# Two K units of every gate and up projection pair in seven products, the residual kept in device memory, and ScalarE's own silu and gelu

## The chip, the core and the metric

The kernel runs on one core of a Trainium2 chip. The metric is the device time of one execution in microseconds (us). The core's engines are TensorE (PE, matrix products; PEld is its weight load), VectorE (DVE), ScalarE (ACT), GpSimd (POOL) and SyncE (SP, which here only issues DMAs). Each engine, and each engine's queue of DMA issues, works through its own list of instructions in order. They wait for each other on semaphores.

## What is computed

Two layers of a gated decoder trunk, all float32, over 256 positions with 2048 channels. Weights are read once.

```python
def reference(x, mix_norm, w_in, ..., w_gate, w_up, w_down):
    for l in range(DEPTH):                       # 2 layers
        h = rms_norm(x, mix_norm[l])
        q, k, v, uv, gate_logits = split(h @ w_in[l])            # 2048 x 7680
        branch_a = sliding_window_attention(rope(norm(q)), rope(norm(k)), v, sinks[l]) @ w_attn_branch[l]
        branch_b = chunked_sgu(jax.nn.gelu(uv), ...) @ w_sgu_branch[l]
        gates = jax.nn.sigmoid(gate_logits)
        x = x + (gates[..., :D] * branch_a + gates[..., D:] * branch_b) @ w_out[l]
        h2 = rms_norm(x, ffn_norm[l])
        x = x + (jax.nn.silu(h2 @ w_gate[l]) * (h2 @ w_up[l])) @ w_down[l]    # 2048 x 5632, 5632 x 2048
    return x
```

## The kernel before

**Work and jobs.** The whole program is a list of jobs. A job multiplies the 256 x K activations by a weight block of 1024 columns (two column blocks of 512, called c = 0 and 1) and runs over K in units of 512. A feed-forward gate or up job has K = 2048, so four units. Activations are held transposed, split into a high and a low float32r part (`uh`, `ul`). Each weight piece is split the same way: ScalarE copies it rounded into `whi` (`high`, L241), VectorE subtracts to get `wlo` (`low`, L249), and TensorE does three matmuls (`three`, L368 to L370): hi x hi, lo x hi, hi x lo.

**Whole units and units in seven products.** A whole unit is four parts (two K halves by two column blocks); one part is 12 matmuls. In a job with `m` units in Strassen form, these come first: seven products `11, t1, t2, 21, t3, 22, t4` of one K half and one column block each, six matmuls a part. Four of the seven need a difference of weight pieces (`add`, L224, VectorE). `Job.m` is the number of such units. With two units the products interleave: 11 of unit 0, 11 of unit 1, t1 of unit 0 and so on. When a product's last unit is done, ScalarE copies one accumulation bank into another (L402): after `11`, after `t2`, and after `t3` into the bank on which `t4` then accumulates. After `21` it copies a bank to `p5`, and after `22` VectorE adds that into two banks (L408). A job in Strassen form holds all five accumulation banks.

**Order.** The order is written by hand: `Stream` hands out the parts and is called for each (`next`, `fill`). It emits splits of up to five parts ahead (N_LOW = 5 `wlo` buffers, N_HIGH = 6 `whi` buffers), and the weight sums some parts further ahead. `after(n, fn)` puts work n slots later (a whole part is one slot, a product half a slot). `evicting` does the work on a finished job's banks: for c = 0 at once, for the second column block spread over the next job.

**Weight loads.** Each unit's 512 x 1024 weights come as two DMAs of 1 MB (the two K halves) into `raw` buffers, of which there are four (N_RAW = 4). SP issues them all (L203), each when the buffer's last reader is done.

**Feed-forward.** Eleven column blocks f in three rounds (0 to 3, 4 to 7, 8 to 10). A round runs a gate job and an up job per pair of f, then two down jobs that add into the residual. Round three ends with one job that holds gate and up of f = 10. `xs` (128 x 2 x 2048) holds the residual in SBUF throughout. The gate eviction is a tanh on ScalarE (L1072) and a multiply on VectorE (L1076); the up eviction is one VectorE multiply (L1084). Gelu in the mixers is a square, a copy, a tanh on ScalarE and two VectorE multiplies.

```python
class Stream:
    def load(self):
        while len(self.raws) < len(loads):
            n = len(self.raws) - N_RAW
            if n >= 0 and last_use[n] >= len(self.parts):
                return
            self.fetch()
```

Of the kernel before, what the change touches and what calls it, by code (L numbers as in the profile page):

```python
# [33 lines left out]
N_RAW = 4  # L34
N_HIGH = 6
N_LOW = 5
N_BIG = 24
G_BUSY, G_LAND = 3.5, 3
T1_LATE, THEN_LATE = 1.5, 3
# [4 lines left out]
M_OUT, M_FFN, M_DOWN = (0, 1), 1, 1  # L44
M_Q = 0
M_GATE, M_ATT, M_SGU = (0, 1, 1, 1), (0, 0), (0, 0)
GELU_A = 0.044715
GELU_C = 0.7978845608028654
# [3 lines left out]
def hybrid_trunk(ctx: ExitStack, tc: tile.TileContext, x, mix_norm, w_in, q_norm, k_norm, sinks,  # L52
# [3 lines left out]

    const = ctx.enter_context(tc.tile_pool(name="const", bufs=1))
# [3 lines left out]
    wsum = ctx.enter_context(tc.tile_pool(name="wsum", bufs=1))  # L61
# [81 lines left out]
    for l in range(DEPTH):  # L143
# [13 lines left out]
        for fs in ROUNDS:  # L157
            for f in fs[::2]:
                if f + 1 < NF:
                    for w in (w_gate, w_up):  # L160
                        add_job([w[l, :, f * CW:(f + 2) * CW]], m=M_FFN)
                else:
                    add_job([w[l, :, f * CW:(f + 1) * CW] for w in (w_gate, w_up)], m=M_FFN)
            for o in (0, CW2):
                add_job([w_down[l, :, o:o + CW2]], units=list(fs), m=M_DOWN)
# [131 lines left out]
    def evicting(c, fn, then=None, ahead=None):  # L297
# [8 lines left out]
        else:  # L306
            late = behind(1, T1_LATE)
# [5 lines left out]
            if then is not None:  # L313
                after(behind(2, THEN_LATE), then)
# [13 lines left out]
    xs = const.tile([P, NT, D], F32, name="xs")  # L328
    for c in range(NCH):
        for t in range(NT):  # L330
            nc.sync.dma_start(xs[:, t, c * CW:(c + 1) * CW],
# [239 lines left out]
    class Norm:  # L571
# [15 lines left out]
        def squares(self, c):  # L587
            for t in range(NT):
                junk = temp(name="junk")
                nc.scalar.activation(junk, xs[:, t, c * CW:(c + 1) * CW], AF.Square,  # L590
                                     accum_out=self.ss[t][:, c:c + 1])

        def unit(self, c, on_pe=False, sums=False, at_once=False):
            transposed(self.units, c, xs[:, :, c * CW:(c + 1) * CW], cols=self.cols[:, 4 * c:4 * c + 4],
                       on_pe=on_pe, sums=sums, at_once=at_once)

        def finish(self):
            self.r, self.rh, self.rr = [], [], []
# [8 lines left out]
            def rest():  # L607
                for t in range(NT):
                    rh = tiny(1, f"rhalf{t}", 2)
                    nc.vector.tensor_scalar(out=rh, in0=self.r[t], scalar1=0.5, scalar2=None, op0=ALU.mult)  # L610
                    rr = tiny(1, f"rr{t}", 2)
                    nc.vector.tensor_tensor(out=rr, in0=self.r[t], in1=rh, op=ALU.mult)
                    self.rh.append(rh)
                    self.rr.append(rr)
# [263 lines left out]
    class Spatial:  # L878
# [6 lines left out]
        def gelu(self, c, ps, dst):  # L885
            sq = slot([P, NT, CW], name="sq")

            def evicted(t):
                nc.scalar.activation(sq[:, t, :], ps[t], AF.Square, scale=self.nrm.r[t])
                nc.scalar.activation(dst[:, t, :], ps[t], AF.Copy, scale=self.nrm.rh[t])  # L890

            def inner():
                nc.vector.scalar_tensor_tensor(out=flat(sq), in0=flat(sq), scalar=1.0 / GELU_A, in1=flat(dst),
                                               op0=ALU.add, op1=ALU.mult)

            def tanh():
                nc.scalar.activation(sq, sq, AF.Tanh, scale=2.0 * GELU_C * GELU_A)

            def outer():
                nc.vector.scalar_tensor_tensor(out=flat(dst), in0=flat(sq), scalar=1.0, in1=flat(dst),  # L900
                                               op0=ALU.add, op1=ALU.mult)

            evicting(c, lambda t: None, ahead=evicted)
            for i, fn in enumerate((inner, tanh, outer)):
                calm(1 + i, fn)
# [56 lines left out]
    def residual(units, nxt, sums, out_at=None, scale=None):  # L962

        for j in range(0, NCH, 2):

            def done(c, ps, j=j):
                o = j + c

                def then():
                    nxt.unit(o, sums=sums and o == 0)  # L970
                    after(5 if c == 0 else 2, lambda: nxt.squares(o))
                    if o == NCH - 1:
                        after(3, lambda: nxt.finish())

                evicting(c, lambda t: added(o, t, ps), then if nxt is not None else None)
# [163 lines left out]
```

## Time and profile before

| | |
|---|---|
| median of 3 runs | 2468.36 us (2466.8 to 2468.55) |
| the profiled execution's own time | 2468.03 us |
| its span, first to last instruction | 2466.3 us |
| busy: PE, PEld, DVE, ACT, POOL | 100%, 82%, 77%, 56%, 19% of the span |
| granted TensorE clock | 1.000 |
| weights and the rest moved by DMA | 507.73 MB, mean 206 GB/s |

A timeline row gives start, length, engine, line, operation, out<-in, and in brackets the idle time before it and who ended it. `x3` means three such instructions in a row. Matmul ends are modelled, so a matmul's own time is read from the distance between two starts.

### The profile page before, as it was taken

How to read it: one execution, taken by the hardware profiler on the slowest of the kernel's cores; microseconds unless marked ns; L12 is line 12 of the kernel's file. 1: busy time of each engine (PE TensorE's matmuls, PEld its weight loads, DVE VectorE, ACT ScalarE, POOL GpSimd, SP SyncE). 2: the span in 40 equal slices, each digit the busy share in tenths (PEclk: the TensorE clock that was granted, in tenths of full speed). 3: DMA queues.
4: the chain of work that ended last, by engine and by line, in shares of the span. 5: the costliest groups of instructions: out<-in, count | busy, mean ns of one | idle time of the engine just before them, and what ended most of it. 6: DMA issues, size and time to landing. Idle time of an engine off the chain costs nothing.

```text
span 2466.3 us, 30726 instructions
## 1 busy us (share of the span) xinstructions
PE 2455.4 (100%) x11046; PEld 2029.3 (82%) x11046; DVE 1887.3 (77%) x2107; ACT 1373.3 (56%) x1688; POOL 470.7 (19%) x903
## 2 busy tenths in 40 slices
PE   9999999999999999999999999999999999999999
PEld 8888888888888888888888888888888888888887
DVE  6797675797977687778867976757878776977696
ACT  6565455476655555555655554544756555655554
POOL 1411300541220022002235022014402200220020
PEclk9999999999999999999999999999999999999999
DMA  8644656766565557566766456566756665665564
GB/s 295 221 156 159 213 172 221 221 217 228 204 220 190 206 204 239 171 229 199 230 235 216 156 169 207 189 195 201 252 187 239 205 208 202 206 223 189 203 205 153
DMA packets 162730, 507.73 MB, mean 206 GB/s; under 512 B 22912, under 2 KB 25584, under 8 KB 162576
## 3 DMA queue, kind: packets, MB, share of 16 engines
q1 hardware_dynamic: 134512, 477.05, 57.7%
q0 software_dynamic: 27744, 28.44, 3.8%
q8 instruction: 86, 1.41, 0.2%
q14 instruction: 68, 0.56, 0.1%
q10 hardware_dynamic: 320, 0.27, 0.0%
HBM read 475.27 MB, written 2.10 MB: 194 GB/s over the span
## 4 chain that ended last, share of the span: by engine, by line
PE 98%; DVE 1%; DMA 0%; ACT 0%; issue 0%; POOL 0%; DVEq 0%; ACTq 0%; POOLq 0%
PE acc L368 32%; PE acc L369 32%; PE acc L370 32%; PE po L864 1%; PE psc L822 1%; DMA tt<-blk 0%; PE ppt L853 0%; PE psg L949 0%; DVE wlo L249 0%; PE pt L533 0%; PE pwarm L346 0%; POOL tt L460 0%; DVE sums L491 0%; DVE blk L454 0%; DVE ul L519 0%
## 5 line engine op out<-in xcount | busy, mean ns | idle before, releaser
L249 DVE TENSOR_TENSOR wlo<-raw,whi 128x1024 fp32r<-128x1024 f32 (+1 forms) x940 | 1132.8, 1218 | 486.1 <-PE acc L369 398.1
L241 ACT ACTIVATE whi<-raw 128x1024 fp32r<-128x1024 f32 (+1 forms) x940 | 983.4, 1057 | 823.1 <-PE acc L370 746.3
L368 PE MATMUL acc<-whi,uh 128*128 128x512 f32 x3164 | 1240.0, 392 | 2.2 <-DVE gate L1043 1.5
L370 PE MATMUL acc<-whi,ul 128*128 128x512 f32 x3164 | 1233.0, 390 | 0.5 <-DVE ul L561 0.5
L369 PE MATMUL acc<-wlo,uh 128*128 128x512 f32 x3164 | 1232.8, 390 | 0.7 <-DVE wlo L249 0.7
L460 POOL DMA_DIRECT2D tt<-blk x800 | 392.2, 497 | 1715.4 <-DVE blk L454 959.7
L368 PEld LDWEIGHTS acc<-whi,uh 128*128 128x128 f32 x3164 | 594.3, 188 | 130.6 <-ACT acc L402 2.7
L370 PEld LDWEIGHTS acc<-whi,ul 128*128 128x128 f32 x3164 | 594.2, 188 | 124.9 <-DVE ul L561 1.0
L369 PEld LDWEIGHTS acc<-wlo,uh 128*128 128x128 f32 x3164 | 594.5, 188 | 122.1 <-DVE wlo L249 1.4
L368 PE MATMUL acc<-whi,sh 128*128 128x512 f32 x336 | 131.0, 390 | 0.8 <-ACT acc L402 0.8
L370 PE MATMUL acc<-whi,sl 128*128 128x512 f32 x336 | 130.9, 390 | 0.0
L369 PE MATMUL acc<-wlo,sh 128*128 128x512 f32 x336 | 130.9, 389 | 0.0
L241 ACT ACTIVATE whi<-sum 128x1024 fp32r<-128x1024 f32 x84 | 89.0, 1059 | 72.7 <-PE acc L370 56.7
L249 DVE TENSOR_TENSOR wlo<-sum,whi 128x1024 fp32r<-128x1024 f32 x84 | 102.6, 1222 | 13.4 <-ACT whi L241 11.0
L402 ACT ACTIVATE acc<-acc 128x512 f32<-128x512 f32 x126 | 74.4, 590 | 21.7 <-PE acc L370 19.8
L368 PEld LDWEIGHTS acc<-whi,sh 128*128 128x128 f32 x336 | 63.1, 188 | 14.3 <-ACT acc L402 1.2
L370 PEld LDWEIGHTS acc<-whi,sl 128*128 128x128 f32 x336 | 63.1, 188 | 13.1
L369 PEld LDWEIGHTS acc<-wlo,sh 128*128 128x128 f32 x336 | 63.1, 188 | 13.0
L561 DVE TENSOR_TENSOR ul<-tt,uh 128x1024 fp32r<-128x1024 f32 x38 | 46.5, 1223 | 34.1 <-ACT uh L558 27.3
L558 ACT ACTIVATE uh<-tt 128x1024 fp32r<-128x1024 f32 x38 | 40.2, 1057 | 43.9 <-DMA tt<-blk 41.3
L408 DVE TENSOR_TENSOR acc<-acc,p 128x512 f32<-128x512 f32 x84 | 54.2, 691 | 0.0
L224 DVE TENSOR_TENSOR sum<-raw,raw 128x1024 f32<-128x1024 f32 x42 | 51.5, 1226 | 1.4
(131 smaller groups left out, 1053.1 us busy)
## 6 DMA issues: line engine op xcount, KB each, us to landing
raw<-in_w_in_dram SPq DMA_DIRECT2D x112, 1024.0 KB, 5.1
raw<-in_w_down_dram SPq DMA_DIRECT2D x88, 1024.0 KB, 6.3
raw<-in_w_gate_dram SPq DMA_DIRECT2D x80, 1024.0 KB, 5.8
raw<-in_w_up_dram SPq DMA_DIRECT2D x80, 1024.0 KB, 5.1
raw<-in_w_out_dram SPq DMA_DIRECT2D x32, 1024.0 KB, 6.7
tt<-blk POOLq DMA_DIRECT2D x800, 32.0 KB, 5.1
raw<-in_w_attn_branch_dram SPq DMA_DIRECT2D x16, 1024.0 KB, 6.4
raw<-in_w_sgu_branch_dram SPq DMA_DIRECT2D x16, 1024.0 KB, 5.6
```

The lines of the kernel that those rows point to most:

```text
L224: nc.vector.tensor_tensor(out=self.raw(dst), in0=self.raw(total[0]), in1=self.raw(total[1]), op=ALU.subtract)
L241: nc.scalar.activation(hi[:, k, :], raw[:, k, :], AF.Copy)
L249: nc.vector.tensor_tensor(out=lo[:, k, :], in0=raw[:, k, :], in1=hi[:, k, :].bitcast(F32), op=ALU.subtract)
L368: nc.tensor.matmul(ps, a, hi, start=first, stop=False, skip_group_check=True)
L369: nc.tensor.matmul(ps, a, lo, start=False, stop=False, skip_group_check=True)
L370: nc.tensor.matmul(ps, b, hi, start=False, stop=last, skip_group_check=True)
L402: nc.scalar.activation({"11": x, "t2": e, "t3": y}[name], a, AF.Copy)
L408: nc.vector.tensor_tensor(out=d, in0=d, in1=fifth, op=ALU.add)
L460: nc.gpsimd.dma_start(blocks(d)[:, :, i] if whole else d[:, i].rearrange("p k t c -> p (k t) c"), src)
L558: nc.scalar.activation(blocks(unit.hi), tv, AF.Copy)
L561: nc.vector.tensor_tensor(out=blocks(unit.lo), in0=tv, in1=blocks(unit.hi).bitcast(F32), op=ALU.subtract)
L822: nc.tensor.matmul(pscore[:, i, :nk], self.qT[pair // 4][j * HD:(j + 1) * HD, pair % 4, t * P:(t + 1) * P], self.kT[j * HD:(j + 1) * HD, : ...
```

## The change

- Gate and up jobs of a column pair have two units in seven products instead of one (`M_FFN = (2, 2, 1)`); the joint job of f = 10 keeps one. There are ten such jobs in each layer. The second unit's activations get their sums too (`sums=o < sums`), and there are two `sum` buffers for weights (N_SUM = 2).
- The residual leaves SBUF. `kept0` to `kept3` are four tiles in device memory. In each residual job SP fetches two 512-column blocks (`fetch_x`, 512 KB each) some slots before they are needed, VectorE adds into them, and SP writes them back (`keep_x`). The room goes to three more general buffers (N_BIG 27) and the second `sum` buffer.
- Silu and gelu are single ScalarE activations; the VectorE multiplies L1076, L893 and L900 and the ScalarE square, copy and tanh go.
- The evictions behind a two-unit job are later: `behind` now picks by the next job's `m`.

```diff
-M_OUT, M_FFN, M_DOWN = (0, 1), 1, 1
+M_OUT, M_FFN, M_DOWN = (0, 1), (2, 2, 1), 1
+N_SUM = 2
-N_BIG = 24
+N_BIG = 27
-T1_LATE, THEN_LATE = 1.5, 3
+T1_LATE, THEN_LATE, UNIT_LATE = (1.5, 3), (3, 7), (3, 3)
...
-                    for w in (w_gate, w_up):
-                        add_job([w[l, :, f * CW:(f + 2) * CW]], m=M_FFN)
+                    for w, m in zip((w_gate, w_up), M_FFN):
+                        add_job([w[l, :, f * CW:(f + 2) * CW]], m=m)
...
-    def behind(whole, strassen):
-        return strassen if job_no[0] < len(jobs) and jobs[job_no[0]].m else whole
+    def behind(*by_units):
+        return by_units[min(jobs[job_no[0]].m if job_no[0] < len(jobs) else 0, len(by_units) - 1)]
...
-            late = behind(1, T1_LATE)
+            late = behind(1, *T1_LATE)
...
+    def fetch_x(c):
+        xt[c] = slot([P, NT, CW], name="x")
+        nc.sync.dma_start(xt[c], rows(home[c]))
+    def keep_x(c):
+        nc.sync.dma_start(rows(kept[c]), xt[c])
+        home[c] = kept[c]
...
+            evicting(c, lambda t: None,
+                     ahead=lambda t: nc.scalar.activation(dst[:, t, :], ps[t], AF.Gelu_apprx_tanh, scale=self.nrm.r[t]))
...
+                if out_at is None:
+                    after(2 if c == 0 else behind(3, 4), lambda: keep_x(o))
...
+            length = 3.5 * job.m + 4 * (len(job.units) - job.m)
+            after(length - 8, lambda j=j: fetch_x(j))
+            after(length - 6, lambda j=j: fetch_x(j + 1))
...
-                    nc.scalar.activation(a[:, t, :], ps[t], AF.Tanh, scale=norm.rh[t])
-                    nc.vector.scalar_tensor_tensor(out=th, in0=th, scalar=1.0, in1=ps[t], op0=ALU.add, op1=ALU.mult)
+                evicting(c, lambda t: None,
+                         ahead=lambda t: nc.scalar.activation(a[:, t, :], ps[t], AF.Silu, scale=norm.r[t]))
```

The places below are all in the first gate job of the second round in layer 0, behind a down job. Its parts are counted from 0. In the changed kernel `raw_1189` and `raw_1194` are unit 0's two K halves, `raw_1203` and `raw_1206` unit 1's; `raw_1241` is the first half of unit 2, the first whole one, and part 14 is its first. L224, L241 and L249 are the same lines in both kernels; L402, L405, L408 are now L417, L420, L423, and the residual add L984 is now L982.

SP before, from this job's first load on (`raw_1156` and `raw_1161` are unit 0, the two after them unit 1, then unit 2):

```order
L203 DMA raw_1156_6352<-in_w_gate_dram 128x2x1024
L203 DMA raw_1161_6386<-in_w_gate_dram 128x2x1024
L203 DMA raw_1168_6436<-in_w_gate_dram 128x2x1024
L203 DMA raw_1172_6456<-in_w_gate_dram 128x2x1024
L203 DMA raw_1192_6570<-in_w_gate_dram 128x2x1024
L203 DMA raw_1193_6572<-in_w_gate_dram 128x2x1024
```

SP in the changed kernel, from unit 0's second half on:

```order
L203 DMA raw_1194_6426<-in_w_gate_dram 128x2x1024
L338 DMA x_1195_6440<-kept2_100 128x2x512
L338 DMA x_1200_6474<-kept3_101 128x2x512
L203 DMA raw_1203_6480<-in_w_gate_dram 128x2x1024
L203 DMA raw_1206_6498<-in_w_gate_dram 128x2x1024
L341 DMA kept2_100<-x_1195_6440 128x2x512
L341 DMA kept3_101<-x_1200_6474 128x2x512
L203 DMA raw_1241_6685<-in_w_gate_dram 128x2x1024
L203 DMA raw_1242_6687<-in_w_gate_dram 128x2x1024
```

Two reads and two writes of the residual now stand between the loads, and the write `kept3<-x_1200` stands ahead of the load of unit 2, which goes into unit 0's buffer.

VectorE before, from the job's third low to the one of its first whole part:

```order
L249 TENSOR_TENSOR wlo_1178_6507<-raw_1156_6352,whi_1175_6488 128x1024
L984 TENSOR_TENSOR xs_92<-acc_1130_6242,xs_92 128x512
L984 TENSOR_TENSOR xs_92<-acc_1132_6244,xs_92 128x512
L249 TENSOR_TENSOR wlo_1180_6525<-raw_1161_6386,whi_1177_6505 128x1024
L249 TENSOR_TENSOR wlo_1187_6546<-raw_1156_6352,whi_1179_6523 128x1024
L984 TENSOR_TENSOR xs_92<-acc_1131_6243,xs_92 128x512
L249 TENSOR_TENSOR wlo_1189_6558<-raw_1161_6386,whi_1186_6544 128x1024
L249 TENSOR_TENSOR wlo_1191_6568<-sum_1171_6454,whi_1188_6556 128x1024
L984 TENSOR_TENSOR xs_92<-acc_1128_6240,xs_92 128x512
L249 TENSOR_TENSOR wlo_1195_6584<-raw_1168_6436,whi_1190_6566 128x1024
```

VectorE in the changed kernel, from the low of part 4 to that of part 10:

```order
L249 TENSOR_TENSOR wlo_1223_6592<-raw_1189_6392,whi_1215_6567 128x1024
L224 TENSOR_TENSOR raw_1189_6392<-raw_1194_6426,raw_1189_6392 128x2x512
L982 TENSOR_TENSOR x_1200_6474<-acc_1164_6282,x_1200_6474 128x512
L249 TENSOR_TENSOR wlo_1225_6604<-raw_1203_6480,whi_1222_6590 128x1024
L224 TENSOR_TENSOR raw_1203_6480<-raw_1206_6498,raw_1203_6480 128x2x512
L249 TENSOR_TENSOR wlo_1227_6616<-raw_1194_6426,whi_1224_6602 128x1024
L249 TENSOR_TENSOR wlo_1229_6626<-raw_1206_6498,whi_1226_6614 128x1024
L224 TENSOR_TENSOR sum_1209_6516<-raw_1194_6426,raw_1189_6392 128x1024
L249 TENSOR_TENSOR wlo_1231_6637<-raw_1189_6392,whi_1228_6624 128x1024
L224 TENSOR_TENSOR sum_1212_6534<-raw_1206_6498,raw_1203_6480 128x1024
L249 TENSOR_TENSOR wlo_1233_6648<-raw_1203_6480,whi_1230_6635 128x1024
L982 TENSOR_TENSOR x_1200_6474<-acc_1161_6279,x_1200_6474 128x512
```

Before, the seven products' sums are done by the third low and only residual adds stand between the lows. Now sums of both units alternate with the lows up to part 9, the low of part 8 is the last reader of unit 0's first buffer, and the last residual add, for which the write of `kept3` waits, stands behind the low of part 9.

ScalarE in the changed kernel, around the copy that follows `t3`:

```order
L241 ACTIVATE whi_1236_6668<-sum_1209_6516 128x1024
L420 ACTIVATE p5_1238_6678<-acc_1218_6586 128x512
L241 ACTIVATE whi_1239_6681<-sum_1212_6534 128x1024
L241 ACTIVATE whi_1243_6695<-raw_1241_6685 128x1024
L417 ACTIVATE acc_1221_6589<-acc_1217_6585 128x512
L241 ACTIVATE whi_1247_6710<-raw_1241_6685 128x1024
```

ScalarE before, at the same copy:

```order
L405 ACTIVATE p5_1196_6592<-acc_1182_6540 128x512
L241 ACTIVATE whi_1197_6594<-raw_1172_6456 128x1024
L402 ACTIVATE acc_1185_6543<-acc_1181_6539 128x512
L241 ACTIVATE whi_1200_6607<-raw_1172_6456 128x1024
L241 ACTIVATE whi_1202_6619<-raw_1192_6570 128x1024
```

The split in front of the copy reads the second weight unit before (`raw_1172`) and the third unit now (`raw_1241`), and the copy fills the bank that part 12 (`t4`) accumulates on. The same holds in every gate and up job of a column pair.

More of the change, by code (lines that the diff above doesn't have):

```diff
@@ L55, in hybrid_trunk @@
     nc = tc.nc
+    dram = ctx.enter_context(tc.tile_pool(name="dram", bufs=1, space=bass.MemoryType.DRAM))
     const = ctx.enter_context(tc.tile_pool(name="const", bufs=1))
@@ L313, in evicting @@
             if then is not None:
-                after(behind(2, THEN_LATE), then)
+                after(behind(2, *late_then), then)
     def tick(n=1, first=None):
@@ L1061, in hybrid_trunk @@
         norm = Norm(ffn_cols(l))
-        residual(mT, norm, M_FFN, scale=0.5)
+        residual(mT, norm, max(M_FFN), scale=0.5)
         nxt = Norm(mix_cols(l + 1)) if l + 1 < DEPTH else None
@@ L1099, in hybrid_trunk @@
             else:
-                residual(hT, None, False)
+                residual(hT, None, 0)
         norm = nxt
```

67 lines of the change are left out of this document (24 added, 43 removed).

## The prediction

> **What bounds the kernel now.** I read the page first: the busy line and the chain that ended last.
>
> ```profile
> span 2466.3 us, 30726 instructions
> PE 2455.4 (100%) x11046; PEld 2029.3 (82%) x11046; DVE 1887.3 (77%) x2107; ACT 1373.3 (56%) x1688; POOL 470.7 (19%) x903
> PE 98%; DVE 1%; DMA 0%; ACT 0%; issue 0%; POOL 0%; DVEq 0%; ACTq 0%; POOLq 0%
> ```
>
> The chain is TensorE for 98%, so matmuls taken away shorten the kernel, as long as nothing else arrives late. Next the timeline of TensorE at the start of an up job, for the price of a part.
>
> ```profile
> 919.34 0.39 PE L368 MATMUL acc<-whi,uh 128*128 128x512 f32 x1
> ...
> 920.70 0.39 PE L368 MATMUL acc<-whi,sh 128*128 128x512 f32 x1
> ...
> 922.06 0.39 PE L368 MATMUL acc<-whi,sh 128*128 128x512 f32 x1
> ```
>
> The rows are the first matmuls of parts 0, 1 and 2: a product of six matmuls takes 1.36 us, 0.227 each, and a whole part of 12 takes 2.72. Then the busy time by job, in one gate, one up and two down jobs.
>
> ```profile
> 877.14:919.34 42.20, 42.20 (x187) 34.95 (x187) 36.94 (x38) 26.50 (x29) 15.09 (x31) 1.00 0.67 224
> 919.34:961.54 42.20, 42.20 (x188) 34.85 (x187) 32.00 (x31) 22.07 (x24) 0.88 (x2) 1.00 0.59 200
> 961.54:1003.70 42.16, 42.16 (x188) 34.92 (x187) 34.37 (x33) 23.59 (x25) 14.78 (x31) 1.00 0.69 224
> ```
>
> Columns are the stretch, its length, and busy us of PE, PEld, DVE, ACT and POOL. VectorE (third) is busy for 37 of 42 us of the gate job. The average hides two regimes, which VectorE's timeline shows:
>
> ```profile
> 908.51 1.22 DVE L249 TENSOR_TENSOR wlo<-raw,whi 128x1024 fp32r<-128x1024 f32 x1 [0.36 <-PE acc L369]
> 909.76 1.22 DVE L224 TENSOR_TENSOR raw<-raw,sum 128x1024 f32<-128x1024 f32 x1
> 910.91 1.22 DVE L224 TENSOR_TENSOR raw<-raw,raw 128x1024 f32<-128x1024 f32 x1
> 912.04 1.22 DVE L249 TENSOR_TENSOR wlo<-sum,whi 128x1024 fp32r<-128x1024 f32 x1
> ...
> 924.20 0.68 DVE L1076 SCALAR_TENSOR_TENSOR hid<-hid,acc 128x512 f32<-128x512 f32 x1
> 924.80 3.49 DVE L249 TENSOR_TENSOR wlo<-raw,whi 128x1024 fp32r<-128x1024 f32 x3
> 928.20 1.29 DVE L408 TENSOR_TENSOR acc<-acc,p 128x512 f32<-128x512 f32 x2
> ...
> 934.37 1.23 DVE L249 TENSOR_TENSOR wlo<-raw,whi 128x1024 fp32r<-128x1024 f32 x1 [1.48 <-PE acc L369]
> ```
>
> In the whole parts VectorE waits about 1.5 us per part for a `wlo` buffer (last row). In the products it runs without a gap: one low per 1.36 us, and sums and evictions besides. By starts, a 1024-wide operation costs 1.14 (910.91 to 912.04), one behind the low it depends on 1.25 (908.51 to 909.76), a 512-wide one 0.60 (924.20 to 924.80). The low at 908.51 is the up job's first (the next one, at 912.04, reads a sum, so it is product t1): VectorE enters a job 919.34 - 908.51 = 10.8 us, or four whole parts, ahead. That lead is all it has for the products.
>
> **What goes.** Two gate and up jobs per pair, five pairs, two layers: 20 units go from 48 to 42 matmuls. 120 x 0.227 = 27.2 us less on TensorE. The rest that goes is not on the chain: VectorE's L1076, and the gelu steps.
>
> **What VectorE gains in work.** A unit in seven products has three lows and four sums more, 7 x 1.14 = 8.0 us; 20 of them are 160 us. L1076 gives back little of it:
>
> ```profile
> L1076 DVE SCALAR_TENSOR_TENSOR hid<-hid,acc 128x512 f32<-128x512 f32 x44 | 28.9, 680 | 0.0
> ```
>
> A job now runs 14 products in 14 x 1.36 = 19.0 us. In that time VectorE must serve lows and sums of twice as many products from the same lead of 10.8 us.
>
> **What the loads gain in waits.** Both split units hold all four `raw` buffers, so the third unit's first load waits for the low of part 8. Before, the unit behind the split one lay in the other two buffers, loaded before the job began. ScalarE's list has the split of that load in front of the copy that part 12 needs, so TensorE needs the load by part 12, two parts before it multiplies with it. The prices:
>
> ```profile
> raw<-in_w_gate_dram SPq DMA_DIRECT2D x80, 1024.0 KB, 5.8
> raw<-in_w_up_dram SPq DMA_DIRECT2D x80, 1024.0 KB, 5.1
> L203 SPq DMA_DIRECT2D raw<-in_w_gate_dram x80: 367/368/368, 512.1 to 2282.8; - x80
> DMA to landing us min/median/max: 3.6/5.6/10.0
> 921.97 1.06 ACT L241 ACTIVATE whi<-sum 128x1024 fp32r<-128x1024 f32 x1
> 922.91 1.06 ACT L241 ACTIVATE whi<-raw 128x1024 fp32r<-128x1024 f32 x1
> 923.86 0.60 ACT L402 ACTIVATE acc<-acc 128x512 f32<-128x512 f32 x1
> ```
>
> A 1 MB load lands 5.1 us after its issue in the up jobs, 5.8 in the busier gate jobs, and 3.6 at the least of all loads; an issue holds SP for 0.37, a split delays what follows by 0.95, the copy takes 0.60. I take 5.1, since no other load is under way when the first of these starts, and add 0.2 as an estimate for the hand-overs (the waits between rows above). So the low of part 8 (or what else frees the load) must be done 5.1 + 0.95 + 0.6 + 0.2 = 6.8 us before part 12, which TensorE reaches at 12 x 1.36 = 16.3. Before, this was no issue:
>
> ```profile
> ACT whi L241 <- DMA raw<-in_w_gate_dram: 1.6, 1, 1.6
> ```
>
> **The jobs one by one**, time 0 being TensorE's first matmul of the job, VectorE starting at -10.8, about 0.8 us included in which it waits for a `wlo` buffer (0.36 at a time, first row above), instructions counted from the order.
>
> Gate job behind a down job (rounds 2 and 3, four in all). To the last residual add: ten lows (11.4), eight sums (four at 1.14, four at 1.25: 9.6), four adds (2.4), in all 24.2 with the idle: it ends at 13.3. Only then does SP issue the write of `kept3`, and behind it the load: 13.3 + 0.4 + 5.1 + 0.2 = 19.0, split and copy to 20.5. TensorE would be there at 16.3. Wait 4.0 us (0.6 of it already in late lows). Four jobs: 16. If the write's 0.5 MB move ahead of the load, at q1's 477.05 MB in 57.7% of 2466 us (0.335 MB per us) that is 1.6 us more.
>
> ```profile
> q1 hardware_dynamic: 134512, 477.05, 57.7%
> ```
>
> Gate job behind w_out (two). As above, plus the two splits and the sums of units 0 and 1 and two pairs of transposes, 4.9 us. The low of part 10 is ready at 18.7 instead of 13.6 (with 0.2 of slack, since the second matmul is the first to read it): 4.9 late. The last residual add ends at 16.3, the copy at 23.5; part 12 at 21.2: 2.3 more. Two jobs at 7.2: 14.
>
> Gate job behind an up job (four). Eleven lows, eight sums, four evictions and two transposes to part 10: 26.6 with idle, done at 15.8, due 13.8: 2.0 late, and the copy 0.3 more. Four at 2.3: 9. VectorE leaves it 2.2 us behind its full lead.
>
> Up job behind that one (four): the lost lead makes its lows 1.1 late and the copy 0.7: four at 1.8, 7. Up job behind the other gate jobs (six): the low of part 8 ends at 9.5 without, 10.2 with an activation split in between, against 9.5 allowed: nothing in four, 0.7 in two, 1.4.
>
> Sum of waits: 16 + 14 + 9 + 7 + 1.4 = 47. The landing bounds it: 3.6 us takes up to 1.5 off each wait for the copy, 15 in all; 5.8 adds 0.7 in about 18 jobs, 12.
>
> **The other edits.** The residual's traffic is 28 writes and 32 reads of 0.5 MB, 31 MB in all against the 477 MB that q1 moved, 7%; the reads stand 8 slots ahead and their buffers' readers are done long before: nothing. Silu in place of tanh has the size of L1072 and reads the same bank: nothing. ScalarE gets ten more table loads:
>
> ```profile
> L343 ACT ACT_TABLE_LOAD x1 | 1.3, 1283 | 1.3 <-PEq L1117 1.3
> 934.54 1.06 ACT L241 ACTIVATE whi<-raw 128x1024 fp32r<-128x1024 f32 x1 [1.65 <-PE acc L370]
> ```
>
> Each costs 1.3 us, and eight of the ten fall in jobs without products, where ScalarE is idle 1.65 us in every part and one to two parts make good for it. Nothing; if all were on the path, 13 us. [...]
>
> **Sum.** 2466.3 - 27.2 + 47 = 2486 for the span, and with the 1.7 us around the span (2468.03) 2488. The profiled execution lies 0.3 us below the median of 2468.36, which changes nothing.
>
> **Rivals.**
> - *The waits stay small, and the kernel is faster.* Place: the product stretch of the 20 jobs. If VectorE's lead lasts and the loads land before the copy is due, only the two heavy gate jobs are late (about 5 each): 2468 - 27 + 10 = 2451. It decides at 1.36 us of wait per job, the gain of six matmuls. For it: four up jobs have no wait in my count, and my lows miss by only 0.6 in the gate jobs behind down jobs. Against it: VectorE's gap-free row group from 924.20 on with one unit only.
> - *Gain and waits cancel.* The lows are late as counted (4.9 x 2 + 0.6 x 4 + 2.0 x 4 + 1.1 x 4 = 25), but the copies aren't: 2466.
> - *The loads come in a crowd.* Four loads of 1 MB are released within about 3 us, next to residual writes. If each lands like w_out's loads, 6.7 us instead of 5.1, the 14 jobs bound by the copy lose 1.6 more: 2510.
>
> ```profile
> raw<-in_w_out_dram SPq DMA_DIRECT2D x32, 1024.0 KB, 6.7
> ```
>
> - *Table loads stop TensorE:* 13 more, 2501.
>
> **Chances.** The forecast 0.52, crowd 0.15, table loads 0.05, faster 0.20, cancel 0.08. Slower by over 0.2% (4.9 us, about what a measurement can tell here) 0.72, within 0.08, faster 0.20. Half of the fast case and less than half of the crowd lie outside a range of 2451 to 2512; the forecast's own, from the landing, is 2473 to 2500.
>
> **What would show it.** In the profile after: 10380 main matmuls, the sum of their three groups by lines; TensorE's idle time in front of L383 to L385 of some 45 us, put down to the copy L417 and to lows L249; ScalarE waiting for DMA `raw<-in_w_gate_dram` and `in_w_up_dram` about 20 times where it was once; SP's writes of `kept3` waiting for VectorE's L982 in six gate jobs. DVE busy should rise to about 2000 us. If ScalarE's waits for these loads are short, or the copy ends before part 11 does, the forecast is wrong at the copy; if VectorE's lows reach part 10 in time, it is wrong at the lead.

## The result and the profile after

The changed kernel takes 2537.65 us (median of 4 runs, 2534.57 to 2543.4) against 2467.58 us: ratio 1.0287 [1.0268, 1.0306], slower by 70 us. The forecast was 2488, slower by 20. The profiled execution took 2537.43 us, its span is 2535.7. From its page, the span, the busy line, the chain that ended last, and two groups of matmuls:

```profile
span 2535.7 us, 30823 instructions
PE 2460.0 (97%) x10926; PEld 2011.9 (79%) x10926; DVE 1994.7 (79%) x2189; ACT 1427.3 (56%) x1736; POOL 471.2 (19%) x903
PE 81%; DMA 8%; DVE 5%; issue 3%; ACT 1%; POOL 1%; SPq 0%; DVEq 0%; ACTq 0%; POOLq 0%
L383 PE MATMUL acc<-whi,uh 128*128 128x512 f32 x2964 | 1167.3, 394 | 30.7 <-ACT acc L417 26.0
L383 PE MATMUL acc<-whi,sh 128*128 128x512 f32 x496 | 195.6, 394 | 4.9 <-ACT acc L417 4.9
```

There are three lines of each kind: 3 x (2964 + 496) = 10380 main matmuls, the 120 fewer that were forecast. Yet TensorE's share of the chain fell from 98% to 81%, and DMA and VectorE stand in it. Next the windows of jobs of layer 0, columns as in the prediction: the gate job behind w_out, the up job behind it, the second gate and up job of the round, and in round two the gate job behind the down job and its up job.

```profile
551.11:606.96 55.85, 44.38 (x181) 34.29 (x180) 47.97 (x52) 35.90 (x49) 16.77 (x34) 0.97 0.54 189
606.96:647.76 40.80, 40.80 (x181) 33.78 (x180) 35.02 (x33) 25.00 (x27) 0.00 (x0) 1.00 0.55 206
647.76:692.08 44.32, 42.47 (x181) 33.31 (x180) 42.34 (x44) 26.93 (x30) 15.74 (x32) 1.00 0.63 214
692.08:735.89 43.81, 42.12 (x181) 33.40 (x180) 41.74 (x40) 26.84 (x30) 0.88 (x2) 1.00 0.52 192
820.22:868.28 48.06, 44.16 (x181) 35.47 (x180) 37.68 (x35) 26.82 (x29) 0.00 (x0) 0.93 0.50 189
868.28:909.08 40.80, 40.80 (x181) 33.78 (x180) 35.38 (x34) 24.89 (x27) 0.00 (x0) 1.00 0.57 206
```

14 products and 8 whole parts are 14 x 1.36 + 8 x 2.72 = 40.8 us, which the second and the last row meet. What a row has beyond 40.8 is extra time: 15.0, 3.5, 3.0 and 7.3 us in the others. The column behind the busy times, the granted clock, is 0.97 and 0.93 in two of them. The waits behind these rows (total, times, longest):

```profile
ACT whi L241 <- DMA raw<-in_w_gate_dram: 100.2, 33, 8.4
ACT whi L241 <- DMA raw<-in_w_up_dram: 68.8, 38, 4.9
PE acc L383 <- ACT acc L417: 30.8, 12, 5.4
PE acc L384 <- DVE wlo L249: 16.9, 29, 2.0
SPq L341 <- DVE x L982: 144.3, 13, 14.4
```

The first row was 1.6 us, once, before. The gate job at 820.22 shows how they follow from each other. SyncE and ScalarE there, from two timelines:

```profile
833.22 0.37 SPq L341 DMA_DIRECT2D kept<-x  x1
833.68 2.40 SPq L203 DMA_DIRECT2D raw<-in_w_gate_dram  x4
839.41 1.06 ACT L241 ACTIVATE whi<-raw 128x1024 fp32r<-128x1024 f32 x1 [6.78 <-DMA raw<-in_w_gate_dram]
840.38 0.58 ACT L417 ACTIVATE acc<-acc 128x512 f32<-128x512 f32 x1
```

The residual write stands in front of the four loads of the third and the fourth unit and goes out when the last residual add is done. The split waits 6.8 us for the first load, and the bank copy behind it starts at 840.4. TensorE's timeline has the rest:

```profile
836.79 0.39 PE L385 MATMUL acc<-whi,sl 128*128 128x512 f32 x1
841.01 0.80 PE L383 MATMUL acc<-whi,uh 128*128 128x512 f32 x1 [3.82 <-ACT acc L417]
841.60 0.63 PE L384 MATMUL acc<-wlo,uh 128*128 128x512 f32 x1
842.03 0.63 PE L385 MATMUL acc<-whi,ul 128*128 128x512 f32 x1
```

Part 12 begins at 841.01, 20.8 us into the job (20.5 forecast). But from there matmuls start 0.43 us apart instead of 0.23. The granted clock (third column from the right) in four windows around it:

```profile
836.46:839.87 3.41, 0.72 (x4) 0.26 (x2) 1.27 (x2) 0.46 (x1) 0.00 (x0) 1.00 1.01 402
839.87:843.28 3.41, 2.27 (x5) 1.83 (x6) 2.55 (x3) 3.41 (x5) 0.00 (x0) 0.50 1.03 420
843.28:846.70 3.42, 3.42 (x9) 2.65 (x8) 3.42 (x5) 1.69 (x2) 0.00 (x0) 0.50 1.02 412
846.70:850.11 3.41, 3.41 (x16) 2.81 (x15) 1.73 (x2) 1.73 (x2) 0.00 (x0) 1.00 1.03 410
```

The granted clock was 0.50 for 6.83 us, from 839.87 to 846.70, the last 1.1 us of the wait included, and 1.00 again behind that. The profiled execution has it at 0.50 in six places, one in each of the six gate jobs behind w_out and down jobs, two of them 3.41 us long and four 6.83; from the starts of the matmuls in them they cost 12.9 us. The kernel before has none up to its last matmul.

The start of the program is longer too. ScalarE's first rows of after, and a wait of TensorE:

```profile
9.91 0.39 ACTq L352 DMA_DIRECT2D first_rows<-in_mix_norm_dram  x1
10.33 1.28 ACT L358 ACT_TABLE_LOAD   x1 [10.33 <-DMA x<-in_x_dram]
PE pf L363 <- DMA first_rows<-in_mix_norm_dram: 10.1, 1, 10.1
```

`first_rows` was issued at 0.80 us before; now it goes out only when a load of x has landed. The diff gives no hint of it: in the source of both kernels its two lines stand behind the loads of x, and only the buffers that x goes into are others. TensorE's first product part starts at 20.2 us instead of 8.6.

### The profile page after: what moved, and what is told of

Read it like the earlier page. It is cut to its first block, busy times and chain, and to the rows that moved or that the text cites. A ratio compares the mean times of both kernels' runs of the same rounds, so it can differ in the third digit from the quotient of the medians.

```text
span 2535.7 us, 30823 instructions
## 1 busy us (share of the span) xinstructions
PE 2460.0 (97%) x10926; PEld 2011.9 (79%) x10926; DVE 1994.7 (79%) x2189; ACT 1427.3 (56%) x1736; POOL 471.2 (19%) x903
## 4 chain that ended last, share of the span: by engine, by line
PE 81%; DMA 8%; DVE 5%; issue 3%; ACT 1%; POOL 1%; SPq 0%; DVEq 0%; ACTq 0%; POOLq 0%
PE acc L383 27%; PE acc L384 26%; PE acc L385 26%; DMA tt<-blk 5%; DVE wlo L249 2%; DMA raw<-in_w_gate_dram 2%; DMA raw<-in_w_up_dram 1%; PE po L876 1%; DVE sum L224 1%; POOL tt L475 1%; PE psc L834 1%; DVE raw L224 1%; ACT whi L241 1%; PE ppt L865 0%; DVE ul L576 0%
## 5 line engine op out<-in xcount | busy, mean ns | idle before, releaser
L249 DVE TENSOR_TENSOR wlo<-raw,whi 128x1024 fp32r<-128x1024 f32 (+1 forms) x960 | 1152.3, 1216 | 440.4 <-PE acc L384 298.7
L241 ACT ACTIVATE whi<-raw 128x1024 fp32r<-128x1024 f32 (+1 forms) x960 | 996.8, 1055 | 814.5 <-PE acc L385 547.8
L383 PE MATMUL acc<-whi,uh 128*128 128x512 f32 x2964 | 1167.3, 394 | 30.7 <-ACT acc L417 26.0
L385 PE MATMUL acc<-whi,ul 128*128 128x512 f32 x2964 | 1157.3, 390 | 5.7 <-DVE ul L576 5.7
L384 PE MATMUL acc<-wlo,uh 128*128 128x512 f32 x2964 | 1157.9, 391 | 3.6 <-DVE wlo L249 3.6
L384 PE MATMUL acc<-wlo,sh 128*128 128x512 f32 x496 | 198.4, 400 | 14.1 <-DVE wlo L249 13.3
L383 PE MATMUL acc<-whi,sh 128*128 128x512 f32 x496 | 195.6, 394 | 4.9 <-ACT acc L417 4.9
L385 PE MATMUL acc<-whi,sl 128*128 128x512 f32 x496 | 194.8, 393 | 0.0
L241 ACT ACTIVATE whi<-sum 128x1024 fp32r<-128x1024 f32 x124 | 131.2, 1058 | 73.2 <-PE acc L385 45.2
L249 DVE TENSOR_TENSOR wlo<-sum,whi 128x1024 fp32r<-128x1024 f32 x124 | 149.3, 1217 | 11.9 <-PE acc L384 5.6
L417 ACT ACTIVATE acc<-acc 128x512 f32<-128x512 f32 x126 | 73.7, 585 | 20.1 <-PE acc L385 19.2
L224 DVE TENSOR_TENSOR raw<-raw,sum 128x1024 f32<-128x1024 f32 x62 | 75.6, 1219 | 0.8
L224 DVE TENSOR_TENSOR sum<-raw,raw 128x1024 f32<-128x1024 f32 x62 | 75.6, 1219 | 0.8
L224 DVE TENSOR_TENSOR sum<-raw 128x1024 f32<-128x1024 f32 x62 | 75.6, 1219 | 0.0
L224 DVE TENSOR_TENSOR raw<-raw,raw 128x1024 f32<-128x1024 f32 x62 | 75.4, 1217 | 0.0
```

The source lines that it names most:

```text
L224: nc.vector.tensor_tensor(out=self.raw(dst), in0=self.raw(total[0]), in1=self.raw(total[1]), op=ALU.subtract)
L241: nc.scalar.activation(hi[:, k, :], raw[:, k, :], AF.Copy)
L249: nc.vector.tensor_tensor(out=lo[:, k, :], in0=raw[:, k, :], in1=hi[:, k, :].bitcast(F32), op=ALU.subtract)
L383: nc.tensor.matmul(ps, a, hi, start=first, stop=False, skip_group_check=True)
L384: nc.tensor.matmul(ps, a, lo, start=False, stop=False, skip_group_check=True)
L385: nc.tensor.matmul(ps, b, hi, start=False, stop=last, skip_group_check=True)
```

## The experiments

All times are medians; "before" ran on the same chip beside them (2467.3 to 2467.7 us).

**The start alone.** From the changed kernel:

```diff
+    first_rows = slot([16, P], name="first_rows")
+    nc.scalar.dma_start(first_rows, mix_norm[0].rearrange("(k p) -> k p", p=P))
     def rows(v):
...
-    first_rows = slot([16, P], name="first_rows")
-    nc.scalar.dma_start(first_rows, mix_norm[0].rearrange("(k p) -> k p", p=P))
```

> The changed kernel, with one edit: the buffer and the DMA of first_rows (on ScalarE's queue) stand ahead of the DMAs of x again, as in the kernel before, where it was issued at 0.80 us. Theory (the program's start is a cost of its own, 11.6 us): first_rows lands before 5 us, TensorE's first product part starts near 8.6 us instead of 20.2, every later job is the same length, and the time falls by 10 to 12 us, to 2526. Rival (the start waits for the x loads themselves, which now go into general buffers): TensorE starts near 20 us as before the edit and the time stays within 2 us of 2537.6.

2530.38 us (2527.18 to 2534.16), ratio 1.0256 [1.0241, 1.0271]. The first part starts at 8.6 us, 11.6 earlier, so the place is shown (whether the buffer or the DMA has to stand in front isn't told apart, since the edit moves both). Only 7.3 us of it arrived: the two gate jobs behind w_out took 18.1 and 17.5 us extra instead of 15.0 and 16.0. The rival is out; the expected time was missed by 4 us.

**The residual write alone.**

```diff
-                    after(2 if c == 0 else behind(3, 4), lambda: keep_x(o))
+                    after(2 if c == 0 else behind(3, 4, 11), lambda: keep_x(o))
```

> The changed kernel, with one edit: the write of the second column block of a residual pair is issued 11 slots into a two-unit job instead of 4, so it stands behind that job's weight loads on SyncE's queue. Theory (the load of the third unit is late because the write ahead of it waits for the last residual add): in the four gate jobs behind down jobs the extra time of TensorE falls from 7.2 us each to 1 to 3, in the two behind w_out from 15.5 to 8 to 11, the half-clock stretches there go with the waits, and the time falls by 25 to 35 us, to about 2508. Rival (VectorE is late itself, so the low that frees the buffer is as late as the residual add): the loads start within 1 us of where they did, and the time falls by less than 6 us.

2511.21 us, ratio 1.0170 [1.0153, 1.0187], 26 us less. SyncE's timeline in the gate job of round two, and the windows of that job and of the one behind w_out:

```profile
828.12 5.51 SPq L203 DMA_DIRECT2D raw<-in_w_gate_dram  x4
817.61:859.30 41.69, 41.43 (x181) 33.55 (x180) 37.23 (x35) 26.08 (x29) 0.00 (x0) 1.00 0.63 222
550.89:603.49 52.60, 45.42 (x181) 35.71 (x180) 46.71 (x51) 35.85 (x49) 16.75 (x34) 0.94 0.58 200
```

The loads begin 10.5 us into the job instead of 13.5, the job has 0.9 us extra instead of 7.3, and its clock is 1.00. All four such gate jobs fall to 0.6 to 0.9 us. So the write in front of the loads cost them their whole wait but the late lows, and the half clock with it. Behind w_out 11.8 and 13.1 us remain, more than expected: there VectorE is late as well, and the half clock stays (0.94 in the last row).

**The copy ahead of the split alone.** `highs` for the first whole part behind two units is handed out after the copy L417, not before it:

```diff
+    behind_copy = set()
+    base = 0
+    for job in jobs:
+        if job.m == 2:
+            behind_copy.add(base + 7 * job.m)
+        base += len(job.steps)
...
-                if len(self.highs) < min(upto + 1, n) and self.summed > len(self.highs):
+                if len(self.highs) < min(upto + (len(self.highs) not in behind_copy), n) and self.summed > len(self.highs):
```

> The changed kernel, with one edit: on ScalarE the split of the first whole part behind two units in seven products is emitted after the bank copy for product t4 instead of before it; nothing else moves. Theory (the copy, not the multiplication, is what the late load holds up): the wait at part 12 goes, and what is left of it shows two products (2.7 us) later, ahead of part 14, where the weights themselves are wanted. Waits of 3 us become 0.5 or less, those of 4.5 us with a half-clock stretch behind them become 1 to 2 us at the full clock. 4 gate jobs behind down jobs save about 5 each, 8 gate and up jobs behind up jobs 2 each, the two behind w_out 4 each: 35 to 45 us in all, to about 2498. Rival (TensorE waits for VectorE's lows at part 10 to 14 anyway): the same waits turn up against L249, and the time falls by under 10 us.

2525.98 us, ratio 1.0236 [1.0221, 1.0251]: 11.7 us less, a third of what was expected. The gate jobs behind down jobs went from 28.6 us in all to 14.3. The jobs behind w_out gained nothing: their wait moved two parts on. And the eight gate and up jobs behind up and gate jobs kept 22.7 of 24.7 us. There the rival is right; most of their waits are for lows, in parts 6 to 10, ahead of the copy.

**One unit everywhere.** `M_FFN = (1, 1, 1)`, the rest of the change kept.

> The changed kernel with M_FFN = (1, 1, 1): gate and up jobs have one unit in seven products, as in the kernel before; the residual in device memory, silu and gelu, the order of the start and the buffers are those of the changed kernel. Theory (the waits come from the second unit alone, and of the rest only the start costs): 2467.6 + 11.6 = 2479, with TensorE's first part near 20 us and waits for weights as short as in the kernel before. Rival (the table loads or the residual's traffic cost TensorE too): 13 us more for the table loads, 2492, or late loads of w_gate in the jobs behind down jobs.

2488.65 us, ratio 1.0087 [1.0072, 1.0102]: 21 us slower than before with the same products, 9.6 more than the start explains. Job by job most of the rest lies in four places: the first w_in job of layer 1 (4.0 us of extra time instead of 0, of which 1.6 are half clock: matmuls start 0.43 us apart there from 1256.58 to 1259.56), the gate jobs behind w_out (2.3 and 4.1 instead of 0 and 3.0), and w_out (0.8). All four are places where the residual is written and its activations are transposed. Gelu's table loads cost TensorE nothing: the first six w_in jobs of layer 0, which hold four of them, have together 34.9 us in which no weights are multiplied, and 35.0 before.

**The three edits together.**

> The changed kernel with the three edits together: first_rows ahead of x, the residual write 11 slots late, and the split behind the copy. Theory (each wait has its own cause, so the parts add): TensorE starts at 8.6 us, gate jobs behind down jobs lose about 0.8 each as with the late write alone, up jobs behind up jobs lose their copy wait of 0.3 to 1.5, and what VectorE's lows cost stays: 2511 - 11.6 - 5 = 2494, still slower than before. Rival (a later start only uncovers another wait, as the gain of 7.3 from 11.6 us suggests): 2500 or more.

2491.93 us, ratio 1.0096 [1.0081, 1.0112]. The parts add up as expected: 19.3 us less than the late write alone, 11.3 of it at the start.

**VectorE's share.** From the kernel with the late write:

```diff
-                evicting(c, upped, lambda: transposed(hT, f, a, ...))
+                evicting(c, lambda t: None, lambda: transposed(hT, f, a, ...))
```

> The kernel with the late residual write, but VectorE's four multiplies of an up job's eviction (0.68 us each, of which two or more fall into the next job's products) are left out, so the hidden activations are silu(gate) alone. Theory (in the gate jobs behind up jobs VectorE's lows are late by its own count of operations, 2.9 us in parts 6 to 10): 2.7 us less of VectorE's work cuts these waits from 3.4 to below 1, and part of the waits of 4.6 in the up jobs behind them, 12 to 18 us in all: 2496. Rival (the lows are late because the loads or the weight buffers come late): the waits stay within 1 us each and the time above 2506.

2499.36 us (one run), 11.9 less; the four multiplies of an up job's eviction are left out here. The windows of the second gate job of round one, with the late write and here:

```profile
644.29:688.86 44.57, 42.38 (x181) 33.32 (x180) 42.27 (x45) 26.65 (x30) 15.69 (x32) 1.00 0.62 213
```

```profile
644.43:686.44 42.01, 41.42 (x181) 33.63 (x180) 39.74 (x41) 27.17 (x31) 15.53 (x32) 1.00 0.63 226
```

Four operations fewer on VectorE, 2.5 us less (third busy column), and 2.6 us less in the job. The gate jobs behind up jobs fell from 13.5 us in all to 4.3, the up jobs behind them from 18.5 to 12.4. So in the gate jobs most of the wait is VectorE's count of operations. In the up jobs a third is shown to be; the rest still lies in parts 6, 8 and 9, which wait for lows, and 0.4 to 1.3 us in part 12, behind the copy.

**Half clock by itself.** In the kernel before, one low in each of ten jobs is computed over and over:

```diff
-            for k in self.pieces(i):
+            for k in [slice(n % 2, n % 2 + 1) for n in range(stalls.get(i, 0))] + self.pieces(i):
                 nc.vector.tensor_tensor(out=lo[:, k, :], in0=raw[:, k, :], ...)
```

> The kernel before, with ten stalls of TensorE of different lengths: in ten jobs one low of a whole part is computed over and over (18 to 33 times half a tile, 0.6 us each, then once whole), which uses up VectorE's lead of 9.6 us and keeps TensorE waiting for about 1 to 10 us. Nothing else differs. Theory (TensorE's half clock in the changed kernel follows from the length of the wait in front of it, whatever its cause): stalls above some 3 us are followed by 3.4 or 6.8 us at a granted clock of 0.5, 1.7 or 3.4 us of extra time each, shorter ones by none: 2467 + 45 + 15 to 20 = 2530. Rival (the half clock comes from the two-unit products or the residual's traffic): the clock stays at 1.0 behind all ten, 2512.

2566.86 us (one run). The stalls came out longer than planned, 1.0 to 16.5 us, in four down jobs with a second wait of 2.6 us for activations queued behind the repeats, so the time says little. The clock says more. Three of the stalls (TensorE's timeline, with the wait in brackets) and the windows that begin with them:

```profile
425.40 0.50 PE L377 MATMUL acc<-wlo,uh 128*128 128x512 f32 x1 [2.21 <-DVE wlo L257]
738.24 0.79 PE L377 MATMUL acc<-wlo,uh 128*128 128x512 f32 x1 [4.00 <-DVE wlo L257]
1693.95 0.79 PE L377 MATMUL acc<-wlo,uh 128*128 128x512 f32 x1 [4.61 <-DVE wlo L257]
425.40:432.40 7.00, 7.00 (x31) 5.76 (x32) 7.00 (x7) 2.13 (x2) 0.00 (x0) 1.00 0.49 132
738.20:752.00 13.80, 11.14 (x40) 8.73 (x41) 10.36 (x9) 4.01 (x4) 0.00 (x0) 0.77 0.59 171
1694.00:1708.00 14.00, 14.00 (x56) 11.49 (x57) 12.81 (x14) 4.25 (x4) 1.75 (x4) 0.90 0.68 231
```

Behind the waits of 1.0 and 2.2 us the granted clock stayed at 1.00. The windows that begin at the end of the eight waits of 4.0 us and more have 0.65 to 0.90; in the one from 738.20 on it was 0.50 up to 744.00. This kernel has neither products of two units nor the residual's traffic, so the rival is out: lows repeated on VectorE, with long waits of TensorE, are enough to bring half clock about (the granted clock is 0.984 over this run, 1.000 before).

**Up jobs alone.** The three edits, and

```diff
-M_OUT, M_FFN, M_DOWN = (0, 1), (2, 2, 1), 1
+M_OUT, M_FFN, M_DOWN = (0, 1), (1, 2, 1), 1
```

> The three edits, and M_FFN = (1, 2, 1): only the up jobs have two units in seven products. Each of the ten up jobs stands behind a gate job with one unit whose eviction asks nothing of VectorE. Theory (VectorE enters these up jobs with its full lead, as in the up jobs of the changed kernel that had no wait): 10 x 1.36 = 13.6 us less on TensorE and no wait in the up jobs; what stays of the other edits is what the run with one unit showed outside the start: 3.4 at the change of layer, 3.4 in the gate jobs behind w_out, 1 in w_out, and 1 to 3 for the second unit's sums there. 2467.4 - 13.6 + 8 + 2 = 2464, faster than before. Rival (14 products in a row outrun VectorE from any lead, 3 to 4 us in each of the ten): 2490.

2468.40 us, ratio 1.0006 [0.9997, 1.0014], 4 us above the expected time. The windows of the gate job behind w_out and the up job behind it:

```profile
539.73:588.63 48.90, 44.10 (x188) 34.37 (x186) 40.54 (x46) 34.22 (x48) 17.11 (x34) 1.00 0.64 215
588.63:629.43 40.80, 40.80 (x182) 33.80 (x180) 38.40 (x36) 25.10 (x27) 0.63 (x2) 1.00 0.57 206
```

No up job waits: ten times 1.36 us is gained in full. It goes back at the places that the kernel with one unit showed, 6.7 and 6.6 us in the gate jobs behind w_out (42.16 is their length without waits; 0 and 3.0 before; 1.5 of the 6.6 are half clock) and 3.2 at the change of layer. Three more kernels take these away in turn.

**The second unit's sums later.**

```diff
-        residual(mT, norm, max(M_FFN), scale=0.5)
+        residual(mT, norm, M_FFN[0], scale=0.5)
+        after(8, lambda nrm=norm: nrm.add_sums(1))
```

> The kernel with two units in the up jobs alone, and one edit more: for the normed activations behind w_out the sums of the second unit are made 8 slots into the gate job that follows, which doesn't need them, instead of in front of it. Theory (these sums sit on VectorE's list in front of that gate job's products): its waits fall from 6.7 and 6.6 us to the 2.3 and 4.1 of the run with one unit everywhere, and the time by 5 to 8 us, to 2462. Rival (the activations come late because the transposes share the DMA engines with the residual): the waits of 2.2 at the job's first part stay, and the time is above 2465.

2464.50 us, ratio 0.9987 [0.9979, 0.9996], 3.9 less where 5 to 8 were expected. The gate jobs behind w_out have 3.2 and 5.3 us of extra time. In the profiled execution the change of layer has 6.0: the wait of 3.2 is the same, but half clock follows it (2.8 us; the granted clock of this execution is 0.998, with the sums in front it is 0.999).

**The writes later.** On top of it `after(12 if c == 0 else 13, lambda: keep_x(o))`.

> As the run with the late sums, and the residual's writes are issued 12 and 13 slots behind their block everywhere instead of 2 to 11, so none runs beside the transposes of the same activations. Theory (the transposes, 32 KB DMAs, land later beside the writes: 5.3 us against 4.5 at the change of layer): the 3.2 us at the change of layer go to 0 or 1, the gate jobs behind w_out gain 1 to 2 each, 5 us in all, to 2457. Rival (it is the reads or the order of the loads): the same time as the run before it within 2 us.

2460.20 us, ratio 0.9971 [0.9960, 0.9982], 4.3 less. The second of these gate jobs has 2.6 us of extra time instead of 5.3. At the change of layer 3.1 are left instead of 6.0, but that is the half clock alone (the job's granted clock is 1.00 instead of 0.93); the waits that the theory was to take away add up to the same 3.1. That the transposes land later for the writes isn't shown either: in the stretch at the change of layer their median is 5.6 us in both kernels.

**The residual back in SBUF.** On top of the late sums:

```diff
-N_BIG = 27
+N_BIG = 23
...
-    xt = [slot([P, NT, CW], name="x") for _ in range(NCH)]
+    xt = [const.tile([P, NT, CW], F32, name=f"x{c}") for c in range(NCH)]
...
-            after(length - 8, lambda j=j: fetch_x(j))
-            after(length - 6, lambda j=j: fetch_x(j + 1))
```

and no `keep_x`.

> As the run with the late sums, but the residual stays in SBUF: four fixed buffers instead of device memory, no reads or writes of it, and 23 general buffers instead of 27 (the same room). Theory (the residual's traffic costs what is left beside the products, and the room it frees isn't needed for up jobs): the change of layer and the gate jobs behind w_out are as in the kernel before, 0, 0 and 3 us of wait, the up jobs have none: 2467.4 - 13.6 = 2454, faster than before by 0.5%. Rival (the room is needed): activations or transposes wait for general buffers, and the time is 2460 or more.

2454.33 us, ratio 0.9946 [0.9932, 0.9960], as expected to within 1 us. The same two jobs:

```profile
539.73:581.89 42.16, 42.16 (x187) 34.92 (x186) 37.47 (x45) 33.09 (x46) 17.48 (x34) 1.00 0.68 225
581.89:622.69 40.80, 40.80 (x181) 33.80 (x180) 38.69 (x37) 25.17 (x27) 0.63 (x2) 1.00 0.56 206
```

The gate job has no wait left, though silu's table load lies in it, and 23 buffers are enough. The one in layer 1 has the 3.0 us of the kernel before, the change of layer 1.3 instead of 0.

**Gate jobs behind down jobs too.** On top of that, `m=2 if f in (4, 8) else m`.

> As the run with the residual in SBUF, and the gate jobs behind down jobs (f = 4 and 8, four in all) have two units too. Theory (without a write in front of their loads they lose only the 0.6 to 0.9 us of late lows seen with the late write, against 1.36 gained): 2 to 3 us less, 2451. Rival (VectorE, with adds of the residual in these jobs, leaves the up job behind them short as well): the up jobs behind them wait 1 to 3 us, and the time is as without the edit or 4 us above.

2450.96 us, ratio 0.9932 [0.9920, 0.9945], the fastest of all. The gate job behind the first down job:

```profile
790.29:831.57 41.28, 41.20 (x182) 33.63 (x180) 37.19 (x35) 26.44 (x29) 0.00 (x0) 1.00 0.56 204
```

0.5 us of extra time against 1.36 gained, in all four, and none in the up jobs behind them.

## Why the prediction was wrong in size

The direction and the path (late lows, the write in front of the loads, the split in front of the copy) were right; 50 of the 70 us were missed. Four steps of the sum make up 44 of them: a wait of TensorE was priced at its own length, without the half clock behind it (12.9), the gate jobs behind w_out got 14 us instead of the 26.5 that they wait (12.5), the program start got nothing (11.6), and the four up jobs behind a late gate job got half of their wait (7.0). Extra time by the prediction's own steps, in us, both layers:

| step | predicted | wait | half clock |
|---|---|---|---|
| 120 matmuls fewer | -27.2 | -27.2 | |
| gate behind a down job, four | 16 | 20.2 | 8.4 |
| gate behind w_out, two | 14 | 26.5 | 4.5 |
| gate behind an up job, four | 9 | 10.7 | |
| up behind that one, four | 7 | 14.0 | |
| up behind the other gate jobs, six | 1.4 | 0 | |
| program start | not in the sum | 11.6 | |
| change of layer, w_out | nothing | 3.9 | |
| wait of 3.0 already in the gate job of layer 1 | not taken off | -3.0 | |
| sum | 20 | 56.7 | 12.9 |

The measured sum of 69.6 meets the difference of the spans, 2535.7 - 2466.3 = 69.4.

- **Gate behind a down job: nearly right.** In the job shown write, load and copy came within 0.3 us of the forecast times (the other three waited up to 1.6 us longer), and the late write took away all but the late lows. The forecast's own figures give a wait of 20.5 - 16.3 = 4.2 us rather than 4.0. What the sum lacked here is the half clock.
- **TensorE's clock: a term that was left out.** The granted clock was 1.000 before, and the sum took a wait to cost its own length. The four waits of 4.5 to 6.1 us behind down jobs cost 6.4 to 7.9. In the profiled execution of the changed kernel the granted clock was 0.50 beside single waits of 3.8, 4.3, 3.8 and 5.4 us in these jobs. In the two jobs behind w_out it was 0.50 beside waits of 0.9 and 2.3 us in layer 0 and of 2.0 and 2.3 us in layer 1, the two of a pair 1.4 us apart. Later in the same two jobs it was 1.00 beside waits of 3.2 and 2.6 us and of 3.0 and 2.6 us (575 to 590 and 1831 to 1845 us). So the length of a wait doesn't tell it alone, and what does isn't shown. The 2 to 4 us of the other gate and up jobs, spread as 0.1 to 1.4 us over parts 4 to 12, stand at a granted clock of 1.00.
- **Gate behind w_out: mis-sized at the lead.** The step let VectorE enter with the 10.8 us of an up job. It doesn't, as ScalarE and VectorE show ahead of that job:

```profile
538.49 1.71 ACT L569 ACTIVATE tt<-tt,vcols 128x256 f32<-128x256 f32 x4 [3.63 <-DMA tt<-blk]
541.18 1.23 DVE L249 TENSOR_TENSOR wlo<-raw,whi 128x1024 fp32r<-128x1024 f32 x1 [3.99 <-ACT whi L241]
```

  ScalarE waits for the transposes of the residual's activations, and VectorE's lows queue behind ScalarE. The first low is ready 6.4 us ahead in layer 0 and 5.3 in layer 1, where other jobs have 9.6. The kernel before had 7.9 and 5.6 there, which the trace of before would have told. A second part of the excess lies where the sum has nothing: 3.8 us in each of these jobs at part 14, the first whole part. TensorE waits there 2.6 us at one stretch for `ul`, the low part of that unit's activations (rows of ScalarE and VectorE in layer 0, and TensorE's waits in the whole run):

```profile
576.91 1.06 ACT L241 ACTIVATE whi<-raw 128x1024 fp32r<-128x1024 f32 x1 [6.93 <-DMA raw<-in_w_gate_dram]
579.33 1.70 ACT L569 ACTIVATE tt<-tt,vcols 128x256 f32<-128x256 f32 x4
584.24 1.22 DVE L576 TENSOR_TENSOR ul<-tt,uh 128x1024 fp32r<-128x1024 f32 x1
PE acc L385 <- DVE ul L576: 5.7, 3, 2.6
```

  ScalarE scales the transposed activations only behind the split that waited for the late load, so the late load holds up the activations too. With the late write, where that load lands earlier, the wait at this place is still 3.2 us: `ul` stands on VectorE's list behind nine lows and additions that run without a gap there. No run takes it away with two units in these jobs. With one unit the late sums and the residual in SBUF bring them back to the 0 and 3.0 us of the kernel before.
- **Up behind that gate job: mis-sized by half.** 3.5 us each instead of 1.8: parts 6, 8 and 9 each wait 0.7 to 0.9 us for their own low, 2.4 us where 1.1 were forecast, and the copy costs 0.4 to 1.4 where 0.7 were. With VectorE's four multiplies left out a third of the wait goes.
- **The other up jobs: right.** No wait in the changed kernel, and at most 1.6 us in single jobs of the later ones.
- **"The other edits: nothing": half wrong.** Table loads cost nothing (34.9 us against 35.0, above). The residual in device memory cost 3.9 us at the change of layer and in w_out and more behind w_out; in the kernel with the late sums it is 10 us in all (2464.50 against 2454.33). The program start cost 11.6, which the prediction doesn't speak of. Why `first_rows` waits for a load of x there stays open.
- **The rivals.** The crowd: gate loads landed in 7.3 us in the median, more than it said, but the first of the four, which decides, took 5.7 in the job shown (833.68 to 839.41) and 6.3 behind w_out in layer 0 (570.64 to 576.91). Against the 5.1 of the sum that is 0.6 and 1.2 us, not the bulk of these waits. The fast case fell at VectorE, which gave out in 10 of 20 jobs. ScalarE waited 71 times for gate and up loads, where some 20 were forecast.

## What to carry to other kernels

A product in fewer matmuls pays only where the engine that prepares its operands enters the job with its full lead; price the jobs one by one and change those alone (here the up jobs and the gate jobs behind down jobs, with the residual back in SBUF: 16.8 us faster instead of 70 slower). Read that lead at each job's own first low, and read the granted clock behind TensorE's waits (here half clock added 12.9 us to them). When a buffer moves, look at the start and the end of the program too, and keep a write that must wait for a late result out of the queue of loads.

## What the hardware showed that was not expected

- In the changed kernel's profiled execution the granted clock was 0.50 for 3.41 or 6.83 us at six places, beside single waits of TensorE of 2.3 to 5.4 us, and 1.00 elsewhere behind the start. Beside waits of 3.2 and 3.0 us of the same execution, and of 2.2 us in the kernel with the repeated lows, it was 1.00.
- The runs of the changed kernel spread over 8.8 us, those of the kernel with the residual in SBUF over 2.3, the 17 runs of the kernel before beside them over 5.0. The granted clocks of the changed kernel's four runs, 0.993, 0.990, 0.990 and 0.992 in the order of the times 2537.43, 2537.87, 2534.57 and 2543.40, don't follow the times; the cause isn't shown.
- A table load of ScalarE between other work took 1.28 us with 0.02 us of idle time in front of it and 0.01 behind, in the eight that came with gelu (the two for silu have 0.34 in front). The one load of the kernel before, with nothing ahead of it on ScalarE, couldn't show this.
